# Second block of a two-block network: the residual's rescaling on VectorE, and the first halves of five output tiles ahead of the attention norm

## The chip, the cores and the metric

The kernel is one program on one core of a Trainium2 chip. The metric is the device time of one execution in microseconds (us); lower is better. Matrix products run on TensorE (PE in the profile, PEld for its weight loads), elementwise work on VectorE (DVE), ScalarE (ACT) and GpSimd (POOL); SyncE (SP) issues the transfers from HBM.

## The reference

Two blocks follow one another on 512 tokens of width 1024. The first has two layers of mixed Fourier, pooling and latent attention. The second is a recurrent and attention block, then cross attention to a memory, then 32 routed experts. The change lies in the first part of the second block:

```python
x = first_block(...)                       # ends in rms_norm(h, final_norm_w)
h = rms_norm_2(x, ln1_w)
proj = h @ w_in
y_rnn = recurrent_group(xr, xg, ...)       # 512 columns
y_att = chunk_band_attention(q, k, v, rel_bias)   # 512 columns, 8 heads
mixed = concat([rms_norm_2(y_rnn, gn_rnn_w), rms_norm_2(y_att, gn_att_w)])
x = x + mixed @ w_out
```

So `x` is needed in two forms: normalised again for `proj`, and as the residual, which is the first block's hidden state times `final_norm_w` times the reciprocal root mean square of each token.

## The kernel before

Activations are kept transposed: eight tiles of 128 channels by 512 tokens (`hT`, `x2(k)` for tile k). Every fp32 product is made of three fp32r matmuls (`mm3`, lines 182 to 185), since both operands are split into a high part (by ACT) and a low part (by DVE for activations, by POOL for weights). A 128x1024 strip of weights is fetched by `weights` (lines 162 to 180) in two pieces of 128x512: a transfer of 256 KB (L172), the high part on ACT (L176), the low part on POOL (L177). Raw, high and low pieces live in pools of four buffers each. `Ahead` (lines 768 to 779) is a list of such fetches; asking for one also writes down the next.

The order of the work on each engine is not the order of the code. A planner of the framework lays the instructions of each engine out when the program is built; what is written earlier goes ahead among what the plan holds ready, and the order is then fixed. Two traits of it show in the rows below: an instruction can run long before its place in the code, and one that is ready can stand behind work that was written ahead of it.

The second block in the order of the code: the value projection with the sums for the norms (lines 811 to 834; `R1` at L834 holds the reciprocal of the first block's last norm, spread over the partitions by `bcast`, whose last step is the copy L729); four input tiles and their convolutions (lines 887 to 896: L890 evacuates, L893 and L895 convolve on DVE, L889 clears four columns on POOL); the gates, gelus and scans of the recurrence, mixed with the query and key projections (line 1047); then lines 1049 to 1052, which rescale the residual in place, eight tiles, first by the norm weight on ACT (L1051), then by `R1` on POOL (L1052). They write no new buffer and wait for nothing but `R1` and the readers of the tile.

The score loop (lines 1054 to 1066) goes over 8 heads and 4 query tiles: scores, softmax (L983 to L986), fillers from a list (projections for the memory), the transposes of the probabilities one step behind (L994), and after a head's fourth tile its outputs (lines 1002 to 1013, PSUM tile `po`), which go to `yat`. Behind the loop: the rest of the fillers (`mem_v` and `rnn_norm`, the latter giving `Y[0..3]`, the recurrent half of the mixed input), the last head's transposes and outputs, then the seam that the change rewrites (lines 1074 to 1086). There the first halves (k = 0 to 3, 12 matmuls) of the output tiles m = 0 and 1 are written ahead of the attention norm; the squares of the four `yat` tiles are summed (L209 on ACT, L211 on DVE), their sums over partitions are taken on PE (`tok_cols`, L713), turned into reciprocal roots (L719 on DVE, L721 on POOL), spread (L727 on PE, L729 on DVE), multiplied in (L1081) and split (L196 on ACT, L197 on DVE) into `Y[4..7]`. Then come the second halves of tiles 0 and 1 and all of tiles 2 to 7, each evacuated onto the residual (L1074, L1085) and prepared for the next norm. The PSUM pool `pm` has three buffers, `ps_` two.

Of the kernel before, what the change touches and what calls it, by code (L numbers as in the profile page):

```python
# [10 lines left out]
F32 = mybir.dt.float32  # L11
# [3 lines left out]
AF = mybir.ActivationFunctionType  # L15
OP = mybir.AluOpType
# [4 lines left out]
KT = D // 128  # L21
S = 512
# [105 lines left out]
def body(ctx, tc, a, out, stop=None, dbg=None):  # L128
    nc = tc.nc
    mm = nc.tensor.matmul  # L130
    ACT = nc.scalar.activation
    V = nc.vector
    G = nc.gpsimd
# [14 lines left out]
    def C(name, l=0):  # L148
        c0, n = _COLS[name, l]
        return cols[:, c0:c0 + n]  # L150
# [31 lines left out]
    def mm3(ps, lh, ll, rh, rl, first, last):  # L182
        mm(ps, lh, rh, start=first, stop=False)  # L183
        mm(ps, lh, rl, start=False, stop=False)  # L184
        mm(ps, ll, rh, start=False, stop=last)  # L185
# [21 lines left out]
    def add_sq(acc, x, n=L, col=1.0, eng=None):  # L207
        sq = slab(n=n)
        ACT(sq, x, AF.Square, scale=col)  # L209
        if acc is not None:  # L210
            (eng or G).tensor_tensor(sq, acc, sq, op=OP.add)  # L211
        return sq


    with ExitStack() as c1:
# [36 lines left out]
        def bcast(r):  # L252

            p = ptt()
            for j in range(5):
                nc.tensor.transpose(p[:, j * 128:j * 128 + 106], r[:106, j:j + 1].to_broadcast([106, 128]),
                                    ident[:106, :106])
            R = slab()
            V.tensor_copy(R[:, :424].rearrange("p (j n) -> p j n", j=4),
                          p[:, :512].rearrange("p (j n) -> p j n", n=128)[:, :, :106])  # L260
            V.tensor_copy(R[:, 422:528], p[:, 512:618])
            return R
# [4 lines left out]
        def proj_g(w, X, evac, small=True, q0=0):  # L267

            K = len(X)
            n = (X[0][0].shape[1] - q0) // 2

            def run(p, hf):
                s = slice(q0 + hf * n, q0 + (hf + 1) * n)
                for k, (xh, xl) in enumerate(X):
                    mm3(p, w[k][0], w[k][1], xh[:, s], xl[:, s], k == 0, k == K - 1)
                    if k % 4 == 3 and k < K - 1:
                        yield

            if small:
                for hf in range(2):
                    p = p1t()[:, :n]
                    yield from run(p, hf)
                    evac(p, lambda t, hf=hf: t[:, hf * n:(hf + 1) * n])
                    yield
            else:
                p = ppt()
                for hf in range(2):
                    yield from run(p[:, hf, :n], hf)  # L290
                evac(p[:, :, :n], halves)
# [362 lines left out]
        class Norm:  # L654


            def __init__(self, w, n, ws=(1.0,)):
                self.w, self.n, self.ws = w, n, ws
                self.X, self.acc = [], [None] * len(ws)
# [29 lines left out]
    def x2(k):  # L689
        return hT[:, k, NM:]  # L690

    xpool = ctx.enter_context(ExitStack())
    with ExitStack() as c2:
# [4 lines left out]
        pm = c2.enter_context(tc.tile_pool(name="pm", bufs=3, space=PSUM))  # L698
        ps_ = c2.enter_context(tc.tile_pool(name="ps", bufs=2, space=PSUM))
# [3 lines left out]
        def sumsq(xs, n=S):  # L703
            acc = None
            for x in xs:
                acc = add_sq(acc, x, n, eng=V)
            return acc

        def tok_cols(acc, nt=4):

            p = px_.tile([128, 512], F32, name="px")
            for j in range(nt):
                mm(p[:, j:j + 1], acc[:, 128 * j:128 * j + 128], ones[:, :1], start=True, stop=True)  # L713
            return p[:, :nt]

        def rsqrt_cols(m, n, nt=4):

            r = sm.tile([128, 4], F32, name="ms")[:, :nt]
            V.tensor_scalar(r, m, 1.0 / n, EPS, op0=OP.mult, op1=OP.add)  # L719
            r2 = sm.tile([128, 4], F32, name="rstd2", bufs=12)[:, :nt]  # L720
            G.tensor_tensor(r2, r, mhalf[:, :nt], op=OP.pow)  # L721
            return r2
# [19 lines left out]
        def run(g):  # L742
            for _ in g:
                pass
# [23 lines left out]
        class Ahead:  # L768


            def __init__(self, todo):
                self.todo, self.ready = todo, {}

            def __call__(self, key):
                i = [t[0] for t in self.todo].index(key)
                for k, f in self.todo[i:i + 2]:
                    if k not in self.ready:
                        self.ready[k] = f()
                return self.ready[key]

        def wcol(src, c0):
            return lambda: weights(KT, [(0, src[:, c0:c0 + 128])])
# [51 lines left out]
        R1 = bcast(r1)  # L834
# [106 lines left out]
        Y = [None] * 8  # L941
# [60 lines left out]
        def outputs(h):  # L1002
            pr = h // 2
            th, tl = PT[h]
            p = po_.tile([128, 512], F32, name="po")
            c = slice(128 * pr, 128 * pr + 128)
            for j in range(4):
                s = slice(384 * j + 128 * j, 384 * j + 512)
                mm3(p[:, 128 * j:], vv[j][0][:, c], vv[j][1][:, c], th[:, s], tl[:, s], j == 0, j == 3)
            if h % 2 == 0:  # L1010
                yat[pr] = slab(n=S)
            r = slice(64 * (h % 2), 64 * (h % 2) + 64)
            ACT(yat[pr][r], p[r], AF.Copy)
# [32 lines left out]
        Rm = bcast(rm, 2)  # L1046
        run(both(main, side, (2, 1)))
        fillers.extend([qk(2), both(qk(3), mem_prep(), (1, 1)), mem_k(), both(mem_v(), rnn_norm(), (2, 1))])
        for k in range(KT):

            ACT(x2(k), x2(k), AF.Identity, scale=C("final_norm_w")[:, k:k + 1])  # L1051
            G.tensor_tensor(x2(k), x2(k), R1, op=OP.mult)  # L1052
        prev = None
        for h in range(8):
            if h + 2 < 8:
                load_bias(h + 2)
            while h not in QK:
                fill()
            for i in range(4):
                e = scores(h, i)  # L1060
                fill(int(STEPS_2[h][i]))
                if prev is not None:
                    transpose_p(*prev)
                    if prev[1] == 3:
                        outputs(prev[0])
                prev = (h, i, e)
        wo = Ahead([(m, wcol(a["w_out_2"][0], 128 * m)) for m in range(8)])
        fill(1000)
        wo(0)
        transpose_p(*prev)  # L1070
        outputs(7)


        outs = [proj_g(wo(m), Y, lambda p, m=m: V.tensor_tensor(x2(m), x2(m), p, op=OP.add)) for m in range(2)]  # L1074
        for g in outs:
            for _ in range(2):
                next(g)
        ya = [yat[k] for k in range(4)]
        Ra = bcast(rsqrt_cols(tok_cols(sumsq(ya)), 512))
        for m in range(4):  # L1080
            V.scalar_tensor_tensor(ya[m], ya[m], C("gn_att_w_2")[:, m:m + 1], Ra, op0=OP.mult, op1=OP.mult)  # L1081
            Y[4 + m] = split(ya[m], n=S)
        nrm = Norm(C("ln2_w_2"), S)
        for m in range(8):
            run(outs[m] if m < 2 else proj_g(wo(m), Y, lambda p: V.tensor_tensor(x2(m), x2(m), p, op=OP.add)))  # L1085
            nrm(m)
        if stop == "b2a":
            nc.sync.dma_start(dbg.rearrange("(k p) t -> p k t", p=128), hT)
# [794 lines left out]
```

## Time and profile before

| | us |
|---|---|
| median of 3 runs | 1425.84 |
| runs | 1422.99, 1425.84, 1426.12 |
| the profiled execution's own time | 1425.72 |
| its span, first to last instruction | 1423.9 |
| PE busy | 1353.4 (95%) |
| DVE, ACT, POOL busy | 683.4, 555.1, 440.1 |

The span is the time of the profiled execution less 1.8 us around it. Times in rows count from the start of the span. A busy PE is not PE at its peak: matmuls overlap, so a matmul of 128x512 that is shown as 0.39 us follows its forerunner by about 0.23 us at the full clock.

### The profile page before, as it was taken

How to read it: one execution, taken by the hardware profiler on the slowest of the kernel's cores; microseconds unless marked ns; L12 is line 12 of the kernel's file. 1: busy time of each engine (PE TensorE's matmuls, PEld its weight loads, DVE VectorE, ACT ScalarE, POOL GpSimd, SP SyncE). 2: the span in 40 equal slices, each digit the busy share in tenths (PEclk: the TensorE clock that was granted, in tenths of full speed). 3: DMA queues.
4: the chain of work that ended last, by engine and by line, in shares of the span. 5: the costliest groups of instructions: out<-in, count | busy, mean ns of one | idle time of the engine just before them, and what ended most of it. 6: DMA issues, size and time to landing. Idle time of an engine off the chain costs nothing.

```text
span 1423.9 us, 21255 instructions
## 1 busy us (share of the span) xinstructions
PE 1353.4 (95%) x8236; PEld 1018.1 (71%) x8236; DVE 683.4 (48%) x1305; ACT 555.1 (39%) x1048; POOL 440.1 (31%) x363
## 2 busy tenths in 40 slices
PE   6999999999999999989999999979999999999996
PEld 5998999999899997767876788863454354354343
DVE  5656775455677636777766244252213123132224
ACT  5355554334555562667755344421111110111113
POOL 3432223743222488464477432512000000000002
PEclk9999999999999999999999999989999999999998
DMA  6321112332211242313345122959999999999994
GB/s 202 96 75 40 49 52 84 97 97 66 56 42 58 69 125 81 90 52 120 103 127 175 38 63 91 347 200 382 423 403 423 422 422 423 422 420 422 422 418 154
DMA packets 159288, 279.32 MB, mean 196 GB/s; under 512 B 15568, under 2 KB 127440, under 8 KB 135120
## 3 DMA queue, kind: packets, MB, share of 16 engines
q1 hardware_dynamic: 159184, 277.92, 53.0%
q8 instruction: 66, 1.08, 0.3%
q14 instruction: 38, 0.31, 0.1%
HBM read 275.79 MB, written 2.10 MB: 195 GB/s over the span
## 4 chain that ended last, share of the span: by engine, by line
PE 59%; DVE 7%; DMA 3%; ACT 2%; issue 1%; POOL 1%; DVEq 0%; SPq 0%; POOLq 0%; ACTq 0%
PE pga L1530 7%; PE pgb L1530 7%; PE pm L184 5%; PE pm L185 5%; PE pm L183 5%; PE pgs L1621 4%; PE pgz L1580 3%; PE pgy L1580 3%; PE pgs L1352 3%; PE p L183 2%; PE p L184 2%; PE p L185 2%; DMA ring<-in_expert_gate_w_dram 1%; DMA ring<-in_expert_up_w_dram 1%; DVE slab L197 1%
## 5 line engine op out<-in xcount | busy, mean ns | idle before, releaser
L177 POOL TENSOR_TENSOR wl<-wraw,wh 128x512 fp32r<-128x512 f32 (+1 forms) x248 | 328.1, 1332 | 457.1 <-ACT wh L176 425.2
L176 ACT ACTIVATE wh<-wraw 128x512 fp32r<-128x512 f32 (+1 forms) x248 | 150.6, 616 | 212.6 <-PE pm L184 49.8
L183 PE MATMUL pp<-slab,wh 128*128 128x264 f32 (+1 forms) x536 | 154.8, 290 | 7.6 <-ACT wh L176 6.8
L184 PE MATMUL pp<-slab,wh 128*128 128x264 f32 (+1 forms) x536 | 155.7, 291 | 2.9 <-DVE slab L204 2.7
L185 PE MATMUL pp<-slab,wl 128*128 128x264 f32 (+1 forms) x536 | 154.8, 289 | 1.0 <-POOL wl L177 1.0
L1788 POOL TENSOR_TENSOR ring<-xtok,sel 128x512 f32<-128x512 f32 x4 | 5.0, 1282 | 406.2 <-DVE xtok L1623 406.2
L185 PE MATMUL pm<-slab,wl 128*128 128x512 f32 (+1 forms) x320 | 121.5, 381 | 5.6 <-POOL wl L177 5.5
L184 PE MATMUL pm<-slab,wh 128*128 128x512 f32 (+1 forms) x320 | 120.9, 378 | 2.2 <-DVE slab L197 2.2
L183 PE MATMUL pm<-slab,wh 128*128 128x512 f32 (+1 forms) x320 | 121.1, 380 | 0.0
L183 PE MATMUL p<-slab,wh 128*128 128x264 f32 (+1 forms) x400 | 115.7, 289 | 3.3 <-DVE rs L247 1.6
L1530 PE MATMUL pga<-ring,xT 128*64 128x512 f32 x504 | 116.1, 596 | 0.0
L1530 PE MATMUL pgb<-ring,xT 128*64 128x512 f32 x512 | 113.7, 592 | 0.3 <-DMA ring<-in_expert_up_w_dram 0.3
L185 PE MATMUL p<-slab,wl 128*128 128x264 f32 (+1 forms) x400 | 113.1, 283 | 0.0
L184 PE MATMUL p<-slab,wh 128*128 128x264 f32 (+1 forms) x400 | 112.8, 282 | 0.0
L183 PEld LDWEIGHTS pp<-slab,wh 128*128 128x128 f32 x536 | 103.6, 194 | 8.0 <-ACT wh L176 6.8
L184 PEld LDWEIGHTS pp<-slab,wh 128*128 128x128 f32 x536 | 103.4, 193 | 4.7 <-DVE slab L204 4.2
L185 PEld LDWEIGHTS pp<-slab,wl 128*128 128x128 f32 x536 | 103.8, 194 | 1.5 <-POOL wl L177 1.5
L1530 PEld LDWEIGHTS pgb<-ring,xT 128*64 128x64 f32 x512 | 37.0, 137 | 73.6 <-issue 71.4
L1590 DVE SCALAR_TENSOR_TENSOR yl<-pgy,wcol,yh 128x512 fp32r<-128x512 f32 x16 | 12.0, 751 | 158.2 <-ACT yh L1589 158.2
L1530 PEld LDWEIGHTS pga<-ring,xT 128*64 128x64 f32 x504 | 35.4, 137 | 66.1 <-issue 65.6
L183 PEld LDWEIGHTS p<-slab,wh 128*128 128x128 f32 x400 | 75.5, 189 | 5.1 <-issue 1.7
L184 PEld LDWEIGHTS p<-slab,wh 128*128 128x128 f32 x400 | 75.4, 189 | 0.0
(412 smaller groups left out, 3007.6 us busy)
## 6 DMA issues: line engine op xcount, KB each, us to landing
ring<-in_expert_gate_w_dram SPq DMA_DIRECT2D x63, 1024.0 KB, 17.7
ring<-in_expert_up_w_dram SPq DMA_DIRECT2D x62, 1024.0 KB, 16.2
ring<-in_expert_down_w_dram SPq DMA_DIRECT2D x56, 1024.0 KB, 17.0
wraw<-in_w_in_dram SPq DMA_DIRECT2D x108, 256.0 KB, 2.9
wraw<-in_w_out_dram SPq DMA_DIRECT2D x48, 256.0 KB, 2.9
wraw<-in_xk_w_dram SPq DMA_DIRECT2D x16, 256.0 KB, 2.9
wraw<-in_xv_w_dram SPq DMA_DIRECT2D x16, 256.0 KB, 2.6
wraw<-in_xq_w_dram SPq DMA_DIRECT2D x16, 256.0 KB, 2.9
```

What stands on the lines that cost most here:

```text
L176: ACT(h, raw, AF.Copy)
L177: G.tensor_tensor(lo, raw, h.bitcast(F32), op=OP.subtract)
L183: mm(ps, lh, rh, start=first, stop=False)
L184: mm(ps, lh, rl, start=False, stop=False)
L185: mm(ps, ll, rh, start=False, stop=last)
L197: V.tensor_tensor(lo, x, h.bitcast(F32), op=OP.subtract)
L1352: mm(p, h3[:, i, 128 * k:128 * k + 128], sl_[i], start=i == 0 and z == 0, stop=i == 3 and z == 1)
L1530: mm(p[64 * z:64 * z + 64], xt[:, k, CAP * (q + z):CAP * (q + z) + 64], W(src, 2 * pr + z, k), start=k == 0, stop=k == KT - 1)
L1580: mm(ps[c // 512][64 * z:64 * z + 64, c % 512:c % 512 + n], hT_[:, k, 64 * z:64 * z + 64], W("d", 2 * pr + z, k, c, n), start=k == 0, stop ...
L1590: V.scalar_tensor_tensor(yl, p, w[:rows, 0:1], yh.bitcast(F32), op0=OP.mult, op1=OP.subtract)
L1621: mm(p, t[:, 128 * i:128 * i + 128], y, start=q == 0, stop=q == len(ys) - 1)
L1788: G.tensor_tensor(y[i][:, :512], xtok[:, i, :512], fnw[:, :512], op=OP.mult)
```

## The change

Three edits in one function. The eight ACT and eight POOL instructions of lines 1049 to 1052 go; in their place one DVE instruction per tile multiplies by the norm weight and by `R1`, written behind the score loop. The squares of `yat` are summed as the heads finish, inside the loop, so that only the last tile's is left behind it. The weights of the output projection are fetched in halves (one piece of 128x512 at a time, in the order in which they are used, with three on the list at once), and the first halves of five output tiles, three in `pm` and two in `ps_`, are written ahead of the attention norm; tiles 5 to 7 follow whole.

```diff
-            def __init__(self, todo):
-                self.todo, self.ready = todo, {}
+            def __init__(self, todo, n=2):
+                self.todo, self.ready, self.n = todo, {}, n
...
-                for k, f in self.todo[i:i + 2]:
+                for k, f in self.todo[i:i + self.n]:
...
-        for k in range(KT):
-
-            ACT(x2(k), x2(k), AF.Identity, scale=C("final_norm_w")[:, k:k + 1])
-            G.tensor_tensor(x2(k), x2(k), R1, op=OP.mult)
-        prev = None
+        prev = acc = None
...
                         outputs(prev[0])
+                        if prev[0] % 2:
+                            acc = add_sq(acc, yat[prev[0] // 2], S, eng=V)
                 prev = (h, i, e)
-        wo = Ahead([(m, wcol(a["w_out_2"][0], 128 * m)) for m in range(8)])
+
+        def whalf(m, hf):
+            return lambda: weights(4, [(0, a["w_out_2"][0][512 * hf:512 * hf + 512, 128 * m:128 * m + 128])])
+
+        NF = 5
+        wo = Ahead([((m, hf), whalf(m, hf)) for ms in (range(NF),) + tuple((m,) for m in range(NF, 8))
+                    for hf in range(2) for m in ms], 3)
+        for k in range(KT):
+
+            V.scalar_tensor_tensor(x2(k), x2(k), C("final_norm_w")[:, k:k + 1], R1, op0=OP.mult, op1=OP.mult)
         fill(1000)
-        wo(0)
+        wo((0, 0))
         transpose_p(*prev)
         outputs(7)
 
 
-        outs = [proj_g(wo(m), Y, lambda p, m=m: V.tensor_tensor(x2(m), x2(m), p, op=OP.add)) for m in range(2)]
-        for g in outs:
-            for _ in range(2):
-                next(g)
+        def out_half(m, hf, p):
+            w = wo((m, hf))
+            for k in range(4):
+                mm3(p, w[k][0], w[k][1], Y[4 * hf + k][0], Y[4 * hf + k][1], hf == 0 and k == 0, hf == 1 and k == 3)
+
+        po = []
+        for m in range(NF):
+            po.append((pm if m < 3 else ps_).tile([128, 512], F32, name="pm" if m < 3 else "ps"))
+            out_half(m, 0, po[m])
         ya = [yat[k] for k in range(4)]
-        Ra = bcast(rsqrt_cols(tok_cols(sumsq(ya)), 512))
+        Ra = bcast(rsqrt_cols(tok_cols(add_sq(acc, ya[3], S, eng=V)), 512))
...
         for m in range(8):
-            run(outs[m] if m < 2 else proj_g(wo(m), Y, lambda p: V.tensor_tensor(x2(m), x2(m), p, op=OP.add)))
+            if m >= NF:
+                po.append(pm.tile([128, 512], F32, name="pm"))
+                out_half(m, 0, po[m])
+            out_half(m, 1, po[m])
+            V.tensor_tensor(x2(m), x2(m), po[m], op=OP.add)
             nrm(m)
```

## Rows read from the trace of the kernel before

**Rows 1.** Busy time by stretch: stretch, us, engines PE to POOL, granted clock, DMA share, GB/s.

```profile
1100.00:1200.00 100.00, 99.31 (x494) 44.94 (x490) 21.16 (x38) 14.34 (x23) 0.00 (x0) 1.00 1.01 422
```

**Rows 2.** Timeline of POOL from 545: start, us, engine, line, operation, idle before.

```profile
548.43 2.54 POOL L1052 TENSOR_TENSOR hT<-hT,slab 128x512 f32<-128x512 f32 x2 [1.24 <-DVE slab L729]
...
552.20 9.07 POOL L1052 TENSOR_TENSOR hT<-hT,slab 128x512 f32<-128x512 f32 x6
...
561.26 4.38 POOL L177 TENSOR_TENSOR wl<-wraw,wh 128x512 fp32r<-128x512 f32 x3
```

**Rows 3.** Timeline of PE from 551.

```profile
559.89 0.39 PE L184 MATMUL pm<-slab,wh 128*128 128x512 f32 x1
562.57 0.50 PE L185 MATMUL pm<-slab,wl 128*128 128x512 f32 x1 [2.29 <-POOL wl L177]
...
563.87 0.63 PE L184 MATMUL pm<-slab,wh 128*128 128x512 f32 x1
...
567.26 0.40 PE L183 MATMUL pm<-slab,wh 128*128 128x512 f32 x1
...
580.19 0.50 PE L184 MATMUL pm<-slab 128*128 128x512 f32 x1
```

**Rows 4.** Busy time of PE on tile pm by stretch: stretch, us, busy (matmuls), clock, DMA.

```profile
749.70:757.54 7.84, 6.00 (x24) 1.00 0.68 200
757.54:769.74 12.20, 8.13 (x29) 1.00 0.68 200
769.74:802.60 32.86, 32.84 (x142) 1.00 0.22 65
```

**Rows 5.** Timeline of PE from 757.

```profile
757.56 1.02 PE L713 MATMUL px<-tab,slab 128*128 128x1 f32 x8
...
759.92 0.65 PE L727 MATMUL px<-tab,rstd 128*128 128x128 f32 x4 [0.76 <-POOL rstd L721]
...
762.81 0.97 PE L183 MATMUL pm<-slab,wh 128*128 128x512 f32 x3
...
769.75 0.50 PE L184 MATMUL pm<-slab,wh 128*128 128x512 f32 x1 [0.51 <-DVE slab L197]
```

**Rows 6.** Single lines: ns minimum/median/maximum, first and last start in us, shapes.

```profile
L895 DVE SCALAR_TENSOR_TENSOR slab<-slab,cols x12: 744/1652/1731, 553.8 to 577.1; 128x512 f32<-128x512 f32 x12
...
L1051 ACT ACTIVATE hT<-hT,cols x8: 712/725/727, 488.9 to 523.5; 128x512 f32<-128x512 f32 x8
...
L1052 POOL TENSOR_TENSOR hT<-hT,slab x8: 1262/1390/1757, 548.4 to 560.0; 128x512 f32<-128x512 f32 x8
...
L893 DVE TENSOR_SCALAR slab<-slab,cols x4: 764/1212/1467, 552.4 to 573.4; 128x512 f32<-128x512 f32 x4
...
L197 DVE TENSOR_TENSOR slab<-slab x52: 410/698/1784, 80.2 to 767.9; 128x528 fp32r<-128x528 f32 x22, 128x512 fp32r<-128x512 f32 x20, 128x256 fp32r<-128x256 f32 x10
```

**Rows 7.** Timeline of DVE from 536.

```profile
551.55 0.69 DVE L890 TENSOR_TENSOR slab<-pm,slab 128x512 f32<-128x512 f32 x1 [3.20 <-PE pm L185]
```

**Rows 8.** Groups of POOL's instructions from 548.4 to 580.2: busy us, mean ns, idle before.

```profile
L177 POOL TENSOR_TENSOR wl<-wraw,wh 128x512 fp32r<-128x512 f32 x9 | 13.0, 1455 | 4.9 <-ACT wh L176 4.9
```

**Rows 9.** Waits from 480 to 510: who waited for whom, us, times, longest.

```profile
PE pp L183 <- ACT slab L196: 0.8, 1, 0.8
```

**Rows 10.** Groups of instructions from 749.7 to 803.

```profile
L211 DVE TENSOR_TENSOR slab<-slab 128x512 f32<-128x512 f32 x3 | 2.8, 918 | 2.6 <-ACT slab L209 2.5
...
L209 ACT ACTIVATE slab<-slab 128x512 f32<-128x512 f32 x4 | 2.3, 624 | 0.0
```

**Rows 11.** Waits of PE from 640 to 727.

```profile
PE px L994 <- DVE slab L986: 3.1, 5, 0.9
```

**Rows 12.** Timelines of DVE and PE: the memory's sum of squares, and its L713.

```profile
534.48 0.43 DVE L814 TENSOR_TENSOR slab<-slab 128x256 f32<-128x256 f32 x1 [4.21 <-POOL slab L211]
...
572.11 0.50 PE L713 MATMUL px<-tab,slab 128*128 128x1 f32 x4
```

**Rows 13.** Timeline of PE from 739: between the two halves of the memory's values.

```profile
739.43 0.50 PE L183 MATMUL pm<-wh,slab 128*128 128x512 f32 x1 [2.18 <-DVE slab L204]
```

## The prediction

> **What bounds the kernel now.** Three views, in this order. The busy time by stretch shows that the expert part, from 1100 us on, keeps PE and the transfers both full [rows 1]. It starts from the buffers that the second block gives back, so a microsecond won or lost on PE's path ahead of it should reach the end whole; no edit touches the expert part itself. Ahead of it PE is the path wherever it is not waiting, so the question is which holes of PE the edits close or open. The timelines show two places.
>
> The first is the residual's rescaling. POOL spends 2.54 us and then 9.07 us on L1052 in one stretch, 548.4 to 561.3; the weights' low parts (L177) stand behind it and come three in a row at 561.26 [rows 2]. PE starts a matmul at 559.89 and the next only at 562.57, released by that L177; then eight matmuls, 563.87 to 567.26, take 3.39 us, about half speed [rows 3].
>
> The second is the seam. Behind the last head's outputs, 24 matmuls of first halves end at 757.54; in the next 12.20 us PE runs 29 on tile `pm`; then it is full, 142 in 32.86 us, which makes 0.2314 us each [rows 4]. In those 12.20 us run the sums over partitions (L713), the reciprocal roots, their spreading (L727), and the four pieces of the attention half, the first usable on PE at 762.81, the last at 769.75 [rows 5]. PE could have run (12.20 - 1.3 for L713 and L727) / 0.2314 = 47; so 18 matmuls, 4.2 us, are lost there.
>
> **The change part by part.** The sum is made against the profiled execution's 1425.72 us, 0.12 below the median of 1425.84.
>
> POOL's rescaling goes. The hole was 562.57 - (559.89 + 0.23) = 2.45 us, the slow stretch cost 3.39 - 8 x 0.2314 = 1.54: **-4.0 us** [rows 3]. What is late next is the first gate's matmul at 580.19, which needs four convolutions and three splits by DVE.
>
> DVE gets eight instructions of two inputs and a scale. Nearest in form is L895: 0.744 us undisturbed, up to 1.731 beside POOL [rows 6]. Where do they run? L1051, written behind the first 1047 lines' work, ran between 488.9 and 523.5, long ahead of its place, since it waited for nothing; L1052 began right when `R1` was there, at 548.4 [rows 6]. The new ones wait for `R1` too and take no buffer, so I expect them in DVE's gaps from 548.4 on, not behind the last scores. DVE is idle there for 3.20 us before 551.55 [rows 7], room for four; each of the next three tiles gives PE 24 x 0.2314 = 5.55 us of work and DVE 0.69 + 0.76 + 3 x 0.74 = 3.7, room for four more. That hides them; but a filler that starts just ahead of a convolution step delays it. I take +0.5 for that. Ends: all eight at 1.731 us (13.8 us) against the 3.20 us idle and the 6.5 us or so that the convolution's twelve steps get back without L1052 beside them (at L895's 1.652 against 0.744 in seven or eight of them): about 4 us on DVE's chain, which eats the whole gain; or nothing lost. So this pair of edits gives **-3.5 us**, between -4.0 and 0.
>
> Here the row shows DVE and POOL slowing one another: L895 took 1.652 us in the median and 0.744 at least [rows 6]. How far do they exclude each other? Undisturbed, twelve L895, four L893 at 0.764, three L197 at 0.698, eight L1052 at 1.262 and nine L177, of the same shape, at as much make 8.9 + 3.1 + 2.1 + 10.1 + 11.4 = 35.6 us [rows 6, 8]; they fitted into 548.4 to 580.2, 31.8 us, so taking turns holds to 0.89. After the change 8 x 0.744 = 6.0 stand for the 10.1: 31.5 us, or 28.0 at 0.89, ending at 576.4: 3.8 us earlier than 580.2, which bears out the -3.5. The Trainium skill (SBUF — State Buffer, "Who interferes with whom") says that a DVE instruction with two SBUF inputs and a GpSimd instruction that reads SBUF exclude one another, the second "fully blocks". By that rule alone the 31.5 us would stand unshortened and end at 579.9, and the sum would lose nearly all of the 3.5; the trace agrees with it in kind, not in full.
>
> ACT loses eight instructions of 0.725 us, 488.9 to 523.5. PE waits for ACT only once there, 0.8 us [rows 9]; I take 0 (ends -0.8 and 0).
>
> Three squares (0.62 us each on ACT) and two additions (0.7 to 1.8 on DVE) move from the seam into the score loop [rows 10]. In the seam they ran beside the outputs and first halves and cost nothing. In the loop PE waits for DVE already, 3.1 us in five places [rows 11]: +0.3, between 0 and +1.5.
>
> The seam. The transfers stay sixteen of 256 KB in SP's queue, and four buffers still carry them: nothing. What decides is where L713 falls, for it is now written behind 60 matmuls rather than 24. A like case: the memory's sum of squares was finished at 534.9, yet its L713 ran at 572.11, behind the 96 matmuls of the four input tiles written ahead of it; not even the hole at 560 let it in [rows 3, 12]. And before the change L713 follows exactly the 24th matmul [rows 4, 5]. So I expect it behind the 60th, 36 x 0.2314 = 8.3 us later, though its input is there as early as before. From then on PE has no first halves left: all five PSUM buffers are taken. It idles but for L727 until the first piece, 762.81 - 757.56 = 5.25 us, and then runs n matmuls in the 6.95 us to the last piece. Against the kernel before, which has 53 done there, it has 60 + n done 8.3 us later: 8.3 - (7 + n) x 0.2314 = 6.7 - 0.2314 n. n was 16 before, with three tiles to draw on; with five there are 15 matmuls for each piece instead of nine, and at most 30 fit. I take n = 22: **+1.6 us**; the ends are n = 30, -0.2, and n = 16, +3.0, the latter with another 1.5 if half speed follows the idle stretch, as it followed the hole of 2.45 us [rows 3].
>
> Sum: -3.5 + 0 + 0.3 + 1.6 = -1.6, so **1424.1 us**.
>
> **The rivals.** *The sums come as soon as they are ready.* If L713 falls among the first halves, 36 more matmuls lie beside the chain; of the 4.2 us lost there about 1 stays, at the last pieces. -3.5 + 0.3 - 3.2 = -6.4: 1419.3 us. For it: PE ran 12 first-half matmuls of tile 2 beside this chain before [rows 4, 5]. Against it: the 37 us that the memory's sums stood ready [rows 12].
>
> *The rescaling runs where it is written*, behind the last scores, slower than before. There PE waits 2.18 us at 739.43 for DVE's evacuation of the memory's values [rows 13], and eight instructions ahead of it add 8 x 0.744 = 6.0. With POOL's full -4.0: -4.0 + 0.3 + 1.6 + 6.0 = +3.9: 1429.6 us. It decides from the third of the eight that falls there. Against it: L1051's early start [rows 6].
>
> *DVE and POOL take strict turns* from 548 to 580, unshortened, 31.5 us, so that the gates start at 579.9, 0.3 earlier than before: -0.3 + 0.3 + 1.6 = +1.6: 1427.3 us. For it: L895's 1.652; against: the 0.89 above. This is the rule cited above at work.
>
> The change may also fail to do what its words say in part: by my forecast the rescaling does not run behind the last scores.
>
> **How the numbers follow.** Forecast 0.6, early sums 0.2, rescaling late 0.09, strict turns 0.11. A measurement of this kernel tells about 0.2%, 2.85 us, from no change, so faster means under 1423.0. The forecast's ends seldom fall together; its own range is 1421.5 to 1427.5, and of its 0.6 I put 0.22 on faster, 0.33 on no change, 0.05 on slower. Early sums give 0.19 and 0.01, late rescaling 0.02 to no change and 0.07 to slower, strict turns 0.01, 0.08 and 0.02. Together 0.42, 0.44, 0.14. The range 1418.0 to 1428.0 leaves out late rescaling, the far third of the early sums and the forecast's tails, some 0.2.
>
> **What would show it.** Right: L1052 gone, no hole of PE near 560 and no half speed after it; the new instructions on DVE from 548 on; the first gate near 576.5; L713 in the seam behind 60 matmuls; then about 4 us of PE without work. Wrong: L713 before the 60th matmul, or the rescaling on DVE after 726; a hole of PE of another cause between 548 and 609; the seam's gain or loss beyond its ends.

## The result, and the profile after

The kernel after the change takes 1433.81 us in the median of four runs (1432.22 to 1434.20); the kernel before, beside it, 1425.45 (four runs, 1422.99 to 1426.12). The ratio is 1.0058 [1.0047, 1.0070]: 8.4 us slower, outside the range of the prediction. The profiled execution took 1434.2 us, its span is 1432.4 against 1423.9 before.

The totals of the page say little. PE is busy for 3.5 us more than before (1353.4), and POOL has lost the 12 us of its rescaling (440.1 before):

```profile
PE 1356.9 (95%) x8236; PEld 1022.1 (71%) x8236; DVE 682.4 (48%) x1313; ACT 550.7 (38%) x1040; POOL 428.1 (30%) x355
```

The loss is found by taking one landmark in each stage from both traces. The first landmark is POOL's split of a weight at 484, ahead of all edited work, for ACT's rescaling (L1051) began at 488.9 [rows 6]. Here the timeline of POOL before, then after:

```profile
484.18 2.54 POOL L177 TENSOR_TENSOR wl<-wraw,wh 128x512 fp32r<-128x512 f32 x2 [16.00 <-ACT wh L176]
```

```profile
484.77 2.56 POOL L177 TENSOR_TENSOR wl<-wraw,wh 128x512 fp32r<-128x512 f32 x2 [16.00 <-ACT wh L176]
```

The execution after is 0.59 us late here already, by nothing that was edited; 0.6 is taken off below. The same split at 546, just ahead of the rescaling on POOL or DVE, is 0.59 us late too (545.87 and 546.46). So the eight instructions that ACT lost in between changed nothing. The score reductions (L983; before, then after) give the stretch of the score loop by their first and last starts:

```profile
L983 DVE CUSTOM_DVE_ANT_0 slab<-ps,slab x32: 265/476/686, 639.4 to 726.1; 128x128 f32<-128x128 f32 x8, 128x256 f32<-128x256 f32 x8, 128x384 f32<-128x384 f32 x8, 128x512 f32<-128x512 f32 x8
```

```profile
L983 DVE CUSTOM_DVE_ANT_0 slab<-ps,slab x32: 267/480/692, 639.9 to 732.6; 128x128 f32<-128x128 f32 x8, 128x256 f32<-128x256 f32 x8, 128x384 f32<-128x384 f32 x8, 128x512 f32<-128x512 f32 x8
```

The seam runs from the last head's transposes (L994) to the last output tile's evacuation (L1085 before, L1101 after). Timelines of PE and DVE before:

```profile
749.43 0.60 PE L994 MATMUL px<-tab,slab 128*128 128x128 f32 x4
...
802.47 0.69 DVE L1085 TENSOR_TENSOR hT<-hT,pm 128x512 f32<-128x512 f32 x1 [3.32 <-PE pm L185]
```

and after:

```profile
756.44 0.60 PE L994 MATMUL px<-tab,slab 128*128 128x128 f32 x4
...
772.77 0.95 PE L713 MATMUL px<-tab,slab 128*128 128x1 f32 x8
...
777.94 1.65 PE L183 MATMUL pm<-slab,wh 128*128 128x512 f32 x3 [2.23 <-ACT slab L196]
...
784.04 0.70 PE L184 MATMUL pm<-slab,wh 128*128 128x512 f32 x2
...
811.19 0.69 DVE L1101 TENSOR_TENSOR hT<-hT,pm 128x512 f32<-128x512 f32 x1 [3.32 <-PE pm L185]
```

Stage by stage: up to the first score 639.4 to 639.9, the offset of 0.6 and nothing more; the score loop 726.1 - 639.4 = 86.7 before, 732.6 - 639.9 = 92.7 after, +6.0; from the loop's end to L994 23.3 and 23.8, +0.5; the seam 802.47 - 749.43 = 53.0 before, 811.19 - 756.44 = 54.8 after, +1.7. With the offset that makes the 8.7 of the last evacuation (811.19 - 802.47), of which 8.5 stand at the end of the span (1432.4 - 1423.9).

So three things are to be explained: why the rescaling's move gains nothing, why three squares and two additions cost 6 us, and the seam. The first shows in the stretch from 548 to 580. Timelines of DVE and of PE after, and PE's L727 before:

```profile
548.98 5.54 DVE L1074 SCALAR_TENSOR_TENSOR hT<-hT,cols,slab 128x512 f32<-128x512 f32 x5
...
558.47 1.78 DVE L1074 SCALAR_TENSOR_TENSOR hT<-hT,cols,slab 128x512 f32<-128x512 f32 x1
...
572.78 0.68 DVE L890 TENSOR_TENSOR slab<-pm,slab 128x512 f32<-128x512 f32 x1
573.38 0.15 DVE L719 TENSOR_SCALAR ms<-px 128x2 f32<-128x2 f32 x1
```

```profile
568.56 0.50 PE L713 MATMUL px<-tab,slab 128*128 128x1 f32 x4
...
574.36 0.43 PE L727 MATMUL px<-tab,rstd 128*128 128x128 f32 x2 [4.04 <-POOL rstd L721]
574.55 0.63 PE L185 MATMUL pm<-slab,wl 128*128 128x512 f32 x1
...
577.97 0.47 PE L184 MATMUL pm<-slab,wh 128*128 128x512 f32 x1
...
580.81 0.39 PE L184 MATMUL pm<-slab 128*128 128x512 f32 x1
```

```profile
575.01 0.43 PE L727 MATMUL px<-tab,rstd 128*128 128x128 f32 x2 [1.14 <-POOL rstd L721]
```

The eight rescaling instructions run where `R1` comes ready, from 548.98 to 560.25, not behind the last scores. PE's hole at 560 [rows 3] is gone, and PE comes to L713 at 568.56 where it came at 572.11 [rows 12]. But DVE has no gap left: it reaches L719 only at 573.38, behind the fourth tile's L890, and PE stands for 4.04 us until the reciprocal root is there, where it stood 1.14 us before. Behind this wait eight matmuls, 574.55 to 577.97, take 3.42 us at a granted clock of 0.52, next to the lower of its two levels (1.2 of 2.4 GHz), as behind the hole of the kernel before, where it was 0.51 [rows 3]. So PE comes to L713 4.1 us earlier without the offset, and loses 2.9 us more at L727 and 3.42 - 8 x 0.2314 = 1.6 behind it: the hole and the slow stretch have moved to another place. The matmul by which the prediction dates the first gate (its L184; its L183 runs a little earlier) is at 580.81, 580.2 without the offset: where it was [rows 3].

### The profile page after: what moved, and what is told of

Same layout as the page of the kernel before. It is cut to its first block, busy times and chain, and to the rows that moved or that the text cites. A ratio compares the mean times of both kernels' runs of the same rounds, so it can differ in the third digit from the quotient of the medians.

```text
span 1432.4 us, 21228 instructions
## 1 busy us (share of the span) xinstructions
PE 1356.9 (95%) x8236; PEld 1022.1 (71%) x8236; DVE 682.4 (48%) x1313; ACT 550.7 (38%) x1040; POOL 428.1 (30%) x355
## 4 chain that ended last, share of the span: by engine, by line
PE 45%; DMA 6%; DVE 5%; ACT 2%; issue 1%; POOL 0%; SPq 0%; DVEq 0%; POOLq 0%; ACTq 0%
PE pgb L1546 7%; PE pga L1546 6%; PE pm L183 4%; PE pm L184 4%; PE pm L185 4%; PE pgs L1637 4%; PE pgz L1596 3%; PE pgy L1596 3%; DMA ring<-in_expert_up_w_dram 3%; PE pgs L1368 3%; DMA ring<-in_expert_gate_w_dram 1%; DMA ring<-in_expert_down_w_dram 1%; PE po L183 1%; PE po L184 1%; PE po L185 1%
## 5 line engine op out<-in xcount | busy, mean ns | idle before, releaser
L177 POOL TENSOR_TENSOR wl<-wraw,wh 128x512 fp32r<-128x512 f32 (+1 forms) x248 | 327.9, 1330 | 477.2 <-ACT wh L176 458.7
L183 PE MATMUL pp<-slab,wh 128*128 128x264 f32 (+1 forms) x536 | 155.0, 290 | 8.1 <-ACT wh L176 7.3
L184 PE MATMUL pp<-slab,wh 128*128 128x264 f32 (+1 forms) x536 | 155.7, 291 | 2.9 <-DVE slab L204 2.6
L183 PE MATMUL pm<-slab,wh 128*128 128x512 f32 (+1 forms) x304 | 116.9, 387 | 3.4 <-ACT slab L196 2.2
L183 PE MATMUL p<-slab,wh 128*128 128x264 f32 (+1 forms) x400 | 115.8, 289 | 3.3 <-DVE rs L247 1.6
L185 PE MATMUL pm<-slab,wl 128*128 128x512 f32 (+1 forms) x304 | 115.2, 382 | 3.3 <-POOL wl L177 3.2
L184 PE MATMUL pm<-slab,wh 128*128 128x512 f32 (+1 forms) x304 | 115.4, 381 | 0.0
L184 PE MATMUL p<-slab,wh 128*128 128x264 f32 (+1 forms) x400 | 112.8, 282 | 0.0
L183 PEld LDWEIGHTS pp<-slab,wh 128*128 128x128 f32 x536 | 103.7, 194 | 8.5 <-ACT wh L176 7.3
L184 PEld LDWEIGHTS pp<-slab,wh 128*128 128x128 f32 x536 | 103.5, 193 | 4.7 <-DVE slab L204 4.2
L183 PEld LDWEIGHTS p<-slab,wh 128*128 128x128 f32 x400 | 75.5, 189 | 5.1 <-issue 1.7
L184 PEld LDWEIGHTS p<-slab,wh 128*128 128x128 f32 x400 | 75.5, 189 | 0.0
```

Source lines behind the costliest of these rows:

```text
L177: G.tensor_tensor(lo, raw, h.bitcast(F32), op=OP.subtract)
```

## The experiments

### Which edit costs what

The change was taken apart first: the squares put back behind the loop in the kernel after, and each edit put alone into the kernel before. `add_sq` makes a square on ACT into a new buffer of the pool `slab` (and adds on DVE); a third way keeps the squares in the loop but writes them into a tile that is no longer used there.

```diff
 # squares back (the kernel after)
-                        if prev[0] % 2:
-                            acc = add_sq(acc, yat[prev[0] // 2], S, eng=V)
...
-        Ra = bcast(rsqrt_cols(tok_cols(add_sq(acc, ya[3], S, eng=V)), 512))
+        Ra = bcast(rsqrt_cols(tok_cols(sumsq(ya)), 512))
```

> The changed kernel with the squares of the attention output summed behind the loop again; the rescaling and the seam stay changed. Theory 1, buffers: the squares cost the loop its 6.0 us (first to last score reduction 86.7 us before the change, 92.7 after), because each takes a buffer of a pool that hands them out in the order of the code, and the scores written behind it are planned behind it. Theory 2, work: the three squares and two additions themselves delay the softmax. Both expect 1433.8 - 6.0 = 1427.8 us and 86.7 us in the loop. Theory 3, plan: another edit upset the loop's order; then 1433.8 us and 92.7 stay.

Measured: 1427.75 us (10 runs), ratio to the kernel before 1.0017 [1.0006, 1.0027]. Some six of the eight microseconds are gone, and the score loop takes 85.8 us in place of 92.7.

The squares alone are the reverse of that diff, put into the kernel before:

> The kernel before with only the squares moved into the loop. Theories 1 and 2: the kernel before + 6.0 us, 1431.4 us, loop 92.7 us. Theory 3: the kernel before, 1425.4 us, loop 86.7.

Measured: 1431.45 us (5 runs), 1.0048 [1.0032, 1.0065], that is +5.6 us by the medians and +6.8 by the ratio; the score reductions run from 637.6 to 729.5, 91.9 us.

```diff
 # squares into a dead tile (the kernel after)
+        def square_m24(k):
+            ACT(m24[:, k], yat[k], AF.Square)
+            if k:
+                V.tensor_tensor(m24[:, 0], m24[:, 0], m24[:, k], op=OP.add)
...
-                            acc = add_sq(acc, yat[prev[0] // 2], S, eng=V)
+                            square_m24(prev[0] // 2)
...
-        Ra = bcast(rsqrt_cols(tok_cols(add_sq(acc, ya[3], S, eng=V)), 512))
+        square_m24(3)
+        Ra = bcast(rsqrt_cols(tok_cols(m24[:, 0]), 512))
```

> The changed kernel with the squares in the loop, but written into a tile that is already there and dead by then (the recurrence's m24) rather than into a new buffer of the shared pool. Same ACT and DVE work as in the changed kernel. Theory 1, buffers: the loss goes, 1427.8 us, loop 86.7 to 88 us. Theory 2, work: it stays, 1433.8 us, loop 92.7. Theory 3: it stays.

Measured: 1428.89 us (10 runs), 1.0021 [1.0010, 1.0032]. The same squares and additions at the same place in the code cost 1428.89 - 1427.75 = 1.1 us when they take no buffer of the pool, which the two intervals don't tell from nothing, and 1433.81 - 1427.75 = 6.1 when they do (5.8 by the ratios, since these two were timed on different chips). The score loop takes 87.8 us here. How it comes about shows in PE's scores (L978) and ACT's timeline. PE before:

```profile
663.33 0.44 PE L978 MATMUL ps<-slab 128*128 128x384 f32 x1
...
665.39 0.48 PE L978 MATMUL ps<-slab 128*128 128x512 f32 x1
```

PE and then ACT in the kernel after:

```profile
663.93 0.44 PE L978 MATMUL ps<-slab 128*128 128x384 f32 x1
...
671.30 0.40 PE L978 MATMUL ps<-slab 128*128 128x512 f32 x1
```

```profile
669.59 0.59 ACT L1013 ACTIVATE slab<-po 64x512 f32<-64x512 f32 x1 [2.55 <-PE po L185]
...
670.75 0.62 ACT L209 ACTIVATE slab<-slab 128x512 f32<-128x512 f32 x1
671.27 0.49 ACT L984 ACTIVATE slab<-slab,st 128x256 f32<-128x256 f32 x1
```

and ACT with the squares in the dead tile (its square is L1050):

```profile
665.05 0.51 ACT L984 ACTIVATE slab<-slab,st 128x256 f32<-128x256 f32 x1 [0.97 <-DVE st L983]
...
669.77 0.62 ACT L1050 ACTIVATE m<-slab 128x512 f32<-128x512 f32 x1
```

Up to the 384-wide score the two kernels differ by the offset; the next score is 7.4 us behind it after, 2.1 before. In the kernel after, an exponential (L984) of 256 columns stands behind the square, and the square behind a head's outputs, for which ACT waits 2.55 us; with the square in another tile the same exponential runs at 665.05, ahead of it all. The scores' buffers come from the same pool as the square's. That a buffer of the pool makes up about 5 of the 6 us is shown by the two runs; that it is the order in which the pool hands its buffers out that holds the later scores back is read from the code and from this order on ACT, and wasn't tried further.

The rescaling alone, on DVE behind the loop, in the kernel before:

```diff
 # rescaling alone (the kernel before)
-        for k in range(KT):
-            ACT(x2(k), x2(k), AF.Identity, scale=C("final_norm_w")[:, k:k + 1])
-            G.tensor_tensor(x2(k), x2(k), R1, op=OP.mult)
...
+        for k in range(KT):
+            V.scalar_tensor_tensor(x2(k), x2(k), C("final_norm_w")[:, k:k + 1], R1, op0=OP.mult, op1=OP.mult)
```

> The kernel before with only the rescaling moved from ACT and POOL to DVE, written behind the loop as in the change. As the changed kernel's trace has it, POOL's hole at 560 goes and PE waits 4.0 us for the memory norm's spreading instead, because DVE is late: 1425.4 us, within 1. My forecast for this edit alone was 1425.4 - 3.5 = 1421.9. If the rescaling upset the loop (theory 3): 1431.

Measured: 1425.33 us (10 runs), 0.9999 [0.9989, 1.0009]: nothing (-0.6 us by the medians, -0.1 by the ratio). PE waits the same 4.04 us at L727.

The seam alone (half tiles of weights, five first halves) in the kernel before; its diff is that part of the change:

> The kernel before with the seam's edit alone (half tiles of weights, five first halves ahead of the attention norm); rescaling and squares as before. Seam 55.4 us rather than 53.0, so 1425.9 + 2.4 = 1428.3 us. If the halves' weights or the rescaling had a part in the seam's time, another value: under 1426.5 the first theory of the seam is in doubt.

Measured: 1427.55 us (10 runs), 1.0017 [1.0007, 1.0026], +1.8. Timelines of PE and DVE:

```profile
749.48 0.60 PE L994 MATMUL px<-tab,slab 128*128 128x128 f32 x4
...
765.88 0.95 PE L713 MATMUL px<-tab,slab 128*128 128x1 f32 x8
...
804.70 0.69 DVE L1100 TENSOR_TENSOR hT<-hT,pm 128x512 f32<-128x512 f32 x1 [3.32 <-PE pm L185]
```

L994 is where it was before, L713 follows it by 16.4 us rather than 8.1 [rows 5], and the seam takes 55.2 us, +2.2. The three edits alone add up to -0.6 + 5.6 + 1.8 = +6.8 by the medians, and to -0.1 + 6.8 + 2.4 = +9.1 by the ratios; the whole change's 8.4 lies between. Taken in turn, from the rescaling (1425.33) to rescaling and seam (1427.75) to all three (1433.81, timed on another chip), they are -0.6, +2.4 and +6.1 against the 1425.89 of the kernel before beside the first two.

### The sums ahead of the last first halves

```diff
 # sums early (squares back, and:)
-        for m in range(NF):
-            po.append((pm if m < 3 else ps_).tile([128, 512], F32, name="pm" if m < 3 else "ps"))
-            out_half(m, 0, po[m])
+
+        def first_halves(ms):
+            for m in ms:
+                po.append((pm if m < 3 else ps_).tile([128, 512], F32, name="pm" if m < 3 else "ps"))
+                out_half(m, 0, po[m])
+
+        first_halves(range(2))
         ya = [yat[k] for k in range(4)]
         Ra = bcast(rsqrt_cols(tok_cols(sumsq(ya)), 512))
+        first_halves(range(2, NF))
```

> The run with the squares behind the loop (e1), with one edit in the seam: the sums over partitions and their spreading are written behind the first halves of two output tiles rather than five; the first halves of tiles 2 to 4 follow them. Same matmuls. Theory A, order: L713 stood behind 60 matmuls and PE ran dry behind it; now it runs behind 24, the other 36 lie beside the chain, and the seam (last transposes to last evacuation, 53.0 us before, 55.4 in e1) falls to about 50: 1422.5 us, 5 below e1 and 3 below the kernel before. Theory B, pieces: the seam is bound by DVE's four pieces whatever lies beside them; then some 53 us and 1425.5.

Measured: 1421.14 us (10 runs, 1419.60 to 1423.35), 0.9968 [0.9957, 0.9978]: faster than both kernels. Timelines of PE and DVE:

```profile
748.16 0.60 PE L994 MATMUL px<-tab,slab 128*128 128x128 f32 x4
...
756.23 0.95 PE L713 MATMUL px<-tab,slab 128*128 128x1 f32 x8
...
797.63 0.69 DVE L1104 TENSOR_TENSOR hT<-hT,pm 128x512 f32<-128x512 f32 x1 [3.32 <-PE pm L185]
```

L713 is 8.1 us behind L994, as before, because it is written behind 24 matmuls again; the 36 others lie beside the chain, and PE waits 0.77 us at L727 and nowhere behind it. The seam takes 49.5 us, 3.6 less than before and 5.3 less than after. Five first halves were the right idea; their place ahead of the sums undid it.

### Why the rescaling gains nothing

Two runs asked what the gates near 580 wait for. The first computes the memory's reciprocal root right behind `R1`, so that L719 is out of the way; the second leaves `R1` to be spread behind the convolutions, with the rescaling on POOL.

```diff
 # the memory's root early (rescaling alone, and:)
         R1 = bcast(r1)
+        rm = rsqrt_cols(tok_cols(macc, 2), D, 2)
+        Rm = bcast(rm, 2)
...
-        rm = rsqrt_cols(tok_cols(macc, 2), D, 2)
-        Rm = bcast(rm, 2)
```

> The run with the rescaling alone (e4), with the memory norm's sums and their spreading moved ahead of the input tiles, so that PE does not wait for them at 570. Theory A, one wait: the 4.0 us that PE waited there was all that ate the rescaling's gain; then the gates start 3 to 4 us earlier and 1425.4 - 3.5 = 1421.9 us. Theory B, DVE is the bound: with eight more instructions DVE finishes the convolutions and the gate's splits no earlier, PE waits for them instead at the first gate, and the time stays at 1425.4, within 1.

Measured: 1425.69 us (10 runs), 1.0002 [0.9993, 1.0012]. The wait of 4.04 us at L727 is gone, and another has its place. Timeline of PE:

```profile
578.97 0.79 PE L184 MATMUL pm<-slab 128*128 128x512 f32 x1 [3.47 <-DVE slab L197]
```

L719 was only the place where PE met a late DVE. This L184 comes 1.4 us earlier than in the run with the rescaling alone (580.38), but from 579.56 to 584.68 the twelve matmuls behind it follow one another every 0.43 us, at a granted clock of 0.50, which costs 2.3; the second tile's L184 is then 1.1 us later (589.23 against 588.13).

```diff
 # R1 late (the kernel before)
-        R1 = bcast(r1)
...
         Rm = bcast(rm, 2)
+        R1 = bcast(r1)
```

> The kernel before with one line moved: the factor R1 that the residual's rescaling waits for is spread behind the convolutions, so that POOL's eight multiplications (unchanged, on POOL) fall among the gates, where POOL is idle two thirds of the time. Theory A: the hole of PE at 560 and the half speed after it go, 4.0 us, and nothing on DVE replaces them: 1425.9 - 3.5 = 1422.4 us. Theory B: L1052 stands ahead of the weights' low parts there too and slows DVE's gates: 1425.9 or more.

Measured: 1427.32 us (10 runs), 1.0014 [1.0004, 1.0024]. POOL's eight products run from 572.6 to 587.1 there, and PE waits in the gates for POOL's weights (2.73 us at 585.46) and for DVE's pieces (2.19 us at 578.27) instead: +1.5.

The last four runs stand on the kernel with the sums early. In the first the rescaling goes back to ACT and POOL; in the second it is left out altogether, so that the run tells of time alone; in the third half of it goes to DVE; in the fourth it is truly put behind the scores.

```diff
 # half on DVE (the rescaling as before, and:)
+            if k < 4:
+                V.scalar_tensor_tensor(x2(k), x2(k), C("final_norm_w")[:, k:k + 1], R1, op0=OP.mult, op1=OP.mult)
+            else:
                 ACT(x2(k), x2(k), AF.Identity, scale=C("final_norm_w")[:, k:k + 1])
                 G.tensor_tensor(x2(k), x2(k), R1, op=OP.mult)
```

```diff
 # truly behind the scores (sums early, and:)
-        R1 = bcast(r1)
...
+        R1 = bcast(r1)
         for k in range(KT):
             V.scalar_tensor_tensor(x2(k), x2(k), C("final_norm_w")[:, k:k + 1], R1, op0=OP.mult, op1=OP.mult)
```

> The rescaling as the kernel before has it (scaling on ScalarE, product on POOL), squares behind the loop, and the seam with the sums written early as in e5. If the move of the rescaling to VectorE is worth nothing, as e4 said (ratio 0.9999): as e5, 1421.1 us, within 1. If the move still cost something that e4 hid: 1 to 2 us less than e5. If it gained the 3.5 us that I had forecast: 1424.6.

Measured: 1421.03 us (6 runs), 0.9968 [0.9954, 0.9982], the same as with DVE's rescaling. The move is worth nothing in this version too.

> As e9, with the second block's rescaling of the residual left out altogether. The most that any placing of the rescaling can give. Theory turns: POOL's eight products of 1.26 go, 10.1 us of the two engines' common time, and the gates begin 4 to 5 us earlier: e9 less 4 to 5, about 1417. Theory VectorE (its own list sets the gates): only what VectorE lost by waiting beside POOL, e9 less 1 to 2, about 1420.

Measured: 1418.11 us (4 runs), 0.9947 [0.9930, 0.9963], 2.9 less. Timelines of DVE and PE with the rescaling on POOL:

```profile
549.41 0.69 DVE L890 TENSOR_TENSOR slab<-pm,slab 128x512 f32<-128x512 f32 x1 [3.21 <-PE pm L185]
...
578.04 0.50 PE L184 MATMUL pm<-slab 128*128 128x512 f32 x1
```

and without it:

```profile
549.76 0.69 DVE L890 TENSOR_TENSOR slab<-pm,slab 128x512 f32<-128x512 f32 x1 [3.20 <-PE pm L185]
550.56 1.31 DVE L893 TENSOR_SCALAR slab<-slab,cols 128x512 f32<-128x512 f32 x1
551.91 3.25 DVE L895 SCALAR_TENSOR_TENSOR slab<-slab,cols 128x512 f32<-128x512 f32 x3
555.30 0.69 DVE L890 TENSOR_TENSOR slab<-pm,slab 128x512 f32<-128x512 f32 x1
...
574.26 0.50 PE L184 MATMUL pm<-slab 128*128 128x512 f32 x1
```

From the first L890 to the first gate it is 28.63 us with POOL's rescaling and 24.50 without: 4.1, the -4.0 that the prediction gave to POOL's hole and what came behind it (2.9 of it show in the median). But see DVE: with nothing added and no L1052 beside it, one tile's work goes from 549.76 to 555.16, 5.40 us, and the next tile's begins at 555.30. PE gives a tile every 5.54 us. The groups of DVE's instructions from 547 to 580, of the kernel before, after, and without rescaling:

```profile
L895 DVE SCALAR_TENSOR_TENSOR slab<-slab,cols 128x512 f32<-128x512 f32 x12 | 15.4, 1287 | 0.4
L893 DVE TENSOR_SCALAR slab<-slab,cols 128x512 f32<-128x512 f32 x4 | 4.7, 1164 | 2.1 <-POOL slab L889 1.9
```

```profile
L895 DVE SCALAR_TENSOR_TENSOR slab<-slab,cols 128x512 f32<-128x512 f32 x12 | 12.9, 1077 | 0.3
L1074 DVE SCALAR_TENSOR_TENSOR hT<-hT,cols,slab 128x512 f32<-128x512 f32 x8 | 8.8, 1140 | 0.0
```

```profile
L895 DVE SCALAR_TENSOR_TENSOR slab<-slab,cols 128x512 f32<-128x512 f32 x12 | 11.8, 979 | 0.4
```

L895 stays at 0.979 us in the mean without any rescaling, since two L177 of each tile still run beside it; 0.744 is what it takes alone. So the room for the eight is the 3.2 us ahead of the first tile and about 0.14 in each of the next three, and they take 8.8. They come out 4.0 us late: L719 starts at 572.8 after, without the offset of 0.6, and at 568.8 without any rescaling, where the execution is 1.8 us early (566.98). In the kernel before it stands at 573.2, for there POOL's list does the like: DVE waits 1.9 us for a clearing of four columns (L889) that stands behind six L1052.

> As e9, but the residual's tiles 0 to 3 are rescaled by one VectorE instruction each, tiles 4 to 7 by ScalarE and POOL. Theory turns (VectorE and POOL take turns and their sum fills the 32 us from 548 to 580): the sum falls by 4 POOL products of 1.26 and rises by 4 VectorE instructions of 0.74, 2.1 us, and the gates begin 1 to 2 us earlier: e9 less 1 to 2, about 1420. Theory VectorE (the gates wait for VectorE's own list): its list grows by 3.0 us while POOL's hole goes: as e9 within 0.7.

Measured: 1422.59 us (10 runs), 0.9977 [0.9967, 0.9986]; not faster than the rescaling all on POOL, if anything 1.6 slower. Timelines of DVE and PE:

```profile
546.57 7.00 DVE L1051 SCALAR_TENSOR_TENSOR hT<-hT,cols,slab 128x512 f32<-128x512 f32 x4
553.49 0.68 DVE L890 TENSOR_TENSOR slab<-pm,slab 128x512 f32<-128x512 f32 x1
...
578.41 0.39 PE L184 MATMUL pm<-slab 128*128 128x512 f32 x1
```

Four instructions on DVE take 7.00 us beside POOL's four, and the first L890 comes some 4 us later than with all eight on POOL (549.41). The two engines' sum, added up from undisturbed durations, has fallen by 2.1 us, and the gates have not moved (580.2 with POOL's rescaling and here, once the offsets of 2.1 and 1.8 us by which these two executions are early are put back): the sum does not decide.

> As e5, but the factor's spreading stands right ahead of the eight rescaling instructions, behind the score loop, so that they run behind the last scores on VectorE, as the change's words have it. Theory cover (VectorE has slack there): e5 less 3 to 4, 1417.5, since 548 to 580 loses the eight instructions on both engines. Theory queue (they stand ahead of the evacuations that the seam waits for): e5 plus 0 to 2.5, the list of 5.9 us at 0.74 each less what 548 to 580 gives back, 1421 to 1423.5.

Measured: 1427.07 us (10 runs), 1.0009 [1.0000, 1.0019], 5.9 more than with the eight at 548, worse than both theories. Timelines of DVE and PE:

```profile
726.50 9.50 DVE L1072 SCALAR_TENSOR_TENSOR hT<-hT,cols,slab 128x512 f32<-128x512 f32 x8
```

```profile
737.87 0.79 PE L183 MATMUL po<-pth,slab 128*128 128x512 f32 x1 [3.83 <-ACT pth L196]
...
758.75 1.02 PE L713 MATMUL px<-tab,slab 128*128 128x1 f32 x8 [2.19 <-DVE slab L211]
```

Near 580 the whole gain is there: the gates begin at 573.60. Behind the scores the eight hold DVE for 9.50 us, ahead of the pieces and evacuations that PE needs; PE stands 3.83 and 2.19 us, and L713 of the seam comes at 758.75 rather than 756.23. (The spreading of `R1`, four L727 and a copy, moves with them.)

## Why the prediction was wrong

**The squares in the loop, +0.3, between 0 and +1.5.** This is the step that failed most: it measured +5.6 alone and +6.1 in the whole, two thirds of the loss. The term was made from the work, 0.62 and 0.7 to 1.8 us, and from PE's waits in the loop [rows 10, 11]. As work it was about right: in the dead tile the same squares cost 1.1 us, within the term's ends. What it left out is that `add_sq` takes a buffer of the pool from which the scores are fed (the way from there to the later scores is read from the code and the order on ACT, as said above), and that a square can't run until a head's outputs are done. The prediction had counted the buffer in the other direction: it noted that the rescaling takes none, and did not ask the same of the squares.

**The rescaling, -3.5, between -4.0 and 0.** It measured between -0.6 and +0.1 (the 1425.33 alone, and 1421.14 against 1421.03), at an end of its range. Where the eight run was right: from 548.98 on, in the gaps that `R1` leaves. The -4.0 for POOL's hole was right too, 4.1 without any rescaling. The part that failed is "that hides them": 3.7 us of DVE's work for each tile of 5.55 was added up from undisturbed durations, and it is 5.40 beside the two L177 that POOL still runs for each tile. Likewise the twelve steps of the convolution got back 15.4 - 11.8 = 3.6 us with no rescaling at all, and 15.4 - 12.9 = 2.5 in the kernel after (L893's four gave 1.5 more there, 3.2 for 4.7), not 6.5. So the end of 0, "which eats the whole gain", came about, though the eight took 8.8 us and not the 13.8 by which it was reached. The estimate by the factor 0.89, which was to bear the -3.5 out, failed with it. ACT's term of 0 was right: 0.59 us of offset at 484 and at 546.

**Strict turns**, the rival at 1427.3, has the right price for this pair (gates 0.3 earlier forecast, none measured), but a sum of both engines' work doesn't foretell the gates: with half the rescaling on either engine it fell by 2.1 us and they stayed, and without any it fell by 10.1 and they came 4.1 us earlier. The rows fit one engine's list at a time, POOL's in front of the weights and of L889, or DVE's in front of L719 and the splits, each lengthened by the other. The Trainium skill (SBUF — State Buffer, "Who interferes with whom") says that a DVE instruction with at most one SBUF input, outside its fast modes, does not contend with GpSimd. The trace agrees: L890, with one operand in PSUM, takes 0.68 to 0.69 us in all the rows above, whatever POOL does beside it.

**The seam, +1.6, between -0.2 and +3.0.** Measured +1.8 alone, +2.4 on top of the rescaling, +1.7 in the trace: right, with the path right and two sizes off that made up for each other, which was luck. L713 was to come 8.3 us later behind the 60th matmul; it came 16.3 behind L994 instead of 8.1, 8.2 later. The first piece was to follow it by 5.25 us; it follows by 5.17. Of the matmuls up to the last piece (784.04) n was 16, not the 22 I took, the worst end of the range, for PE came out of its idle stretch at half speed: it was busy from 777.94 on, but up to 782.80 the granted clock was 0.50. At 0.2314 each these 6.1 us hold at most 26. The prediction had named that half speed as a further 1.5, beside n = 16; here it is what kept n at 16. Six matmuls fewer cost 1.4 us, and that the last piece comes 11.3 us behind L713 rather than 12.2 gives 0.9 back: 8.2 - 0.9 - (7 + 16) x 0.2314 = 2.0.

**Early sums**, the rival at 1419.3, is not what the change does, and L713 showed it. Written into the code it is the best version that still rescales: its seam gains 3.6 us, where the rival said 3.2.

**Rescaling late** did not happen either. As a kernel of its own it gave back the 4.0 and more: from 1418.11 with no rescaling to 1427.07 it costs 9.0 us in that place (7.5 by the profiled spans, 1415.3 and 1422.8), where the rival had 6.0 for eight undisturbed instructions; they took 9.50 us beside POOL.

The sum fails by the rescaling and by the squares: 0 + 6 + 1.7 in place of -3.5 + 0.3 + 1.6. The forecast's mechanism of the seam stands; the larger part of the loss came from a term to which the prediction gave a few words.

## What to carry to other kernels

Before a helper is moved into a loop, ask what it takes besides engine time: a buffer of a pool that the loop itself lives on can put later work behind it, and here the same instructions cost 6.1 us with it and 1.1, hardly told from nothing, without. Room on an engine is to be counted with the durations that it has beside its neighbours once the edit is made, not with its fastest ones: 5.40 us of 5.54 looked like 3.7 of 5.55. And when more work is written ahead of a latency chain to hide it, the chain's own first instruction has to stay ahead of that work; the same five halves cost about 2 us when all are written ahead of the chain and gain 3.6 us when three of them are written behind its first step.

## What the runs showed of the hardware that I had not expected

Which of two instructions on DVE and POOL is lengthened depended, in the pairs looked at, on which began first, and an instruction with one tensor operand and a column of factors takes part in it like one with two. Timelines of DVE and of POOL in the kernel after:

```profile
563.53 0.55 DVE L893 TENSOR_SCALAR slab<-slab,cols 128x512 f32<-128x512 f32 x1
```

```profile
563.75 1.47 POOL L177 TENSOR_TENSOR wl<-wraw,wh 128x512 fp32r<-128x512 f32 x1 [1.48 <-ACT wh L176]
```

L893 began first and took 0.55 us; POOL's product, begun 0.22 us later, took 1.47. In the kernel without rescaling L177 began first, at 550.29, and took 1.30, and L893, from 550.56, took 1.31. The prediction had taken 0.764 as L893's undisturbed time [rows 6].

PE's clock fell in the seam of the kernel after, which the prediction had only as a possibility. Two stretches of its busy time (stretch, us, busy of PE, PEld, DVE, ACT, POOL, granted clock, DMA):

```profile
772.76:779.39 6.63, 3.06 (x16) 2.43 (x15) 3.77 (x7) 1.89 (x3) 2.24 (x2) 0.75 0.43 125
779.39:784.58 5.19, 5.19 (x17) 3.94 (x15) 3.75 (x4) 3.45 (x6) 3.52 (x3) 0.66 0.73 194
```

PE is busy for 3.06 of 6.63 us around L713 and L727, and in the next 5.19 us, though it is full, the granted clock is 0.66 in the mean, between the two levels of 1.2 and 2.4 GHz: matmuls follow one another every 0.43 us up to 782.8, then every 0.23. Taken by themselves, the stretch from 777.94 to 782.80 has 0.50, the lower level, and the one from 782.80 to 784.04 has 0.95. With the sums early there is no such wait, and the granted clock is 1.00 over the whole seam, 748.0 to 797.6.
